# A two-layer hybrid encoder on one core: the softmax of the global branch in one pass, and where a few side operations stand

## The chip, the cores and the metric

The kernel runs on one core of a Trainium2 chip. The metric is device time in microseconds (us), the median of several executions; lower is better. The engines are TensorE (PE in the profile, with its weight loads as PEld), VectorE (DVE), ScalarE (ACT), GpSimd (POOL), and SyncE (SP), which here only issues DMAs. SBUF is the on-chip memory that all of them read; PSUM holds the sums that PE makes, in banks of 512 float32 columns.

## The reference

What is computed: two layers, each with one wide input projection, a grouped-query attention over all tokens, a neighbourhood attention in a window of 8 x 16 grid cells, and merge gates. There are 512 grid tokens and 16 meta tokens, the model is 1024 wide, and heads are 64 wide.

```python
def gqa_attention(q, k, v):
    scale = HEAD_DIM ** -0.5                       # 0.125
    def attend(qb):                                # a block of queries, against all 528 keys
        s = jnp.einsum('bqkgd,bskd->bkgqs', qb, k).astype(jnp.float32) * scale
        p = jax.nn.softmax(s, axis=-1).astype(v.dtype)
        return jnp.einsum('bkgqs,bskd->bqkgd', p, v)
...
def hybrid_layer(x, norm_g, w_in, q_norm_g, k_norm_g, rpb, w_o_attn, w_o_na, w_out, cos, sin):
    h = rms_norm(x, norm_g)
    proj = jnp.einsum('bld,de->ble', h, w_in)
    qa, ka, va, za, qb, kb, vb, zb, ga, gb = split_cols(proj)
    qa = apply_axial_rope(rms_norm(qa.reshape(b, l, ATTN_HEADS, HEAD_DIM), q_norm_g), cos, sin)
    ka = apply_axial_rope(rms_norm(ka.reshape(b, l, ATTN_KV_HEADS, HEAD_DIM), k_norm_g), cos, sin)
...
    oa = gqa_attention(qa, ka, va) * jax.nn.silu(za)
    ob = neighbourhood_attention(qb, kb, vb, rpb) * jax.nn.silu(zb)
    ya = jnp.einsum('ble,ed->bld', oa, w_o_attn)
    yb = jnp.einsum('ble,ed->bld', ob, w_o_na)
    mixed = jax.nn.sigmoid(ga) * ya + jax.nn.sigmoid(gb) * yb
    return x + jnp.einsum('bld,de->ble', mixed, w_out)
```

Everything is in float32.

## The kernel before

**The backbone.** All activations lie with features on the partitions and tokens along the columns. A projection (`product`, L277) makes 128 output features at a time: for each of eight blocks of input features three matmuls, L286 to L288, because weights and activations are split into a rounded high part and the rest (names ending in h and l, or hi and lo), and the product is high x high + high x low + low x high. The sum grows in a bank of the pool `ps_p` (two banks, named pp in the profile). A weight arrives by DMA (`raw`), ACT casts its high part (`whi`, L216) and GpSimd subtracts it for the low one (`wlo`, L217). A layer with 528 tokens runs each chunk as two halves of 264 columns, and where only the 512 grid tokens count, as one run of 512.

**The side work.** The attention branches are cut into short steps that are slipped between the projections. `product` calls `tick` after each half, and the two queues `side_na` (window heads) and `side_gqa` (global units) run what is due at that tick; tables (GQA_AT, NA_AT, NORM_AT at the top of the file) give the tick of each step within its unit, and `later(n, part)` puts a part n ticks on. A scheduler then sets the order on each engine from dependences and this order of code; `tc.high_priority()` lifts an instruction, and `tc.issue_after(x)` holds one behind x.

**The global branch.** A unit is one head and 256 queries: two softmaxes of 128 queries each (`softmax`, L697). PE writes the scores of 128 queries against 528 keys to S, the one tile of the pool `ps_s`, two banks wide (L499, L500, keys in KA0h/KA0l and so on). DVE takes the negated maximum of a row (L704) and multiplies it by the query's factor, a column of `r8` (L705; `r` in the profile); ACT reads S for the exponential with that factor and that maximum, writes P to SBUF and sums the row (L706); DVE inverts the sum (L708) and scales P (L709). PE transposes P (L116) into banks of the pool `ps_t` (two banks, named pt, ptm, and ta, tb, tc, vtb, vtd for other work that takes turns in them); ACT and DVE split a transposed bank into high and low part (`split`, L172 and L173, or `split_down`, L691 and L692), and PE sums with the values (L746). There are 64 softmaxes over both layers.

**The window branch.** A window head writes its scores to the same S, as Sb (called from L817), and its softmax is the one of L821 to L827: for each of four pieces, one DVE pass adds the bias, writes to SBUF and keeps the minimum, and ACT then does the exponential in SBUF. At the end of a head `sums` (L876) multiplies with the values, and `combine` (L672) adds the two halves of the result: ACT copies one half (L676), DVE adds (L677). After every second head `gated` (L679) multiplies by the gate and splits.

**The norms of queries and keys.** `head_roots` (L574) finds the inverse roots for all heads; `pair_factors` (L562) spreads those of the keys to 128 x 512 and 128 x 128 tiles (pfk, pfkm), and later those of the meta queries (pfq), by a copy on DVE (L566). PE transposes them (L601, L604) and DVE multiplies the keys by them (L602, L605). `stack_soon` (L481) then splits the keys of both pairs of heads, high part on ACT (L489), low part on DVE (L490), and two DMAs move what must lie on the other partitions. The projection of the window keys, `kb`, leaves its accumulator through DVE (L933 to L939), the queries `qb` through L943, and the gates through L663 (ACT then does the tanh, L664, and DVE a product, L669, that stands behind the newest maximum).

Of the kernel before, what the change touches and what calls it, by code (L numbers as in the profile page):

```python
# [18 lines left out]
P = 128  # L19
# [72 lines left out]
def trunk_kernel(ctx: ExitStack, tc: tile.TileContext, xT, w, gn, gf, bias, rope, out):  # L92
# [37 lines left out]
    nc.vector.memset(one, 1.0)  # L130
    nc.scalar.activation(one, one, AF.Exp)
    minus_half = cpool.tile([P, 1], F32, name="minus_half")
    nc.vector.memset(minus_half, -0.5)
# [137 lines left out]
    side_na, side_gqa = Side(NA_AT_TICK), Side(GQA_AT_TICK)  # L271

    def tick():
        side_na.tick()
        side_gqa.tick()

    def product(l, c, rhs, full, halves=(0, 1), name="pp", spans=None):  # L277
# [124 lines left out]
    for l in range(DEPTH):  # L402
# [77 lines left out]

        def stack_soon(tag, name, k, n):  # L481

            pairs = []
            for hh, r in enumerate((up, down)):
                kh, kl = slot(tag, f"{name}h{hh}", F32R), slot(tag, f"{name}l{hh}", F32R)
                for to in (up, down):
                    if hh and to is up:
                        continue
                    nc.scalar.copy(kh[to, :n], k[r, :n])  # L489
                    nc.vector.tensor_sub(kl[to, :n], k[r, :n], kh[to, :n].bitcast(F32))  # L490
# [71 lines left out]
        def pair_factors(t, c, n, name):  # L562

            f = slot("G", f"pf{name}{l}") if n > 1 else tiny.tile([P, P], F32, tag="pf", bufs=1, name=f"pf{name}{l}")
            f = f[:, :P * n].rearrange("p (n h d) -> p n h d", n=n, h=2)
            nc.vector.tensor_copy(f, st["r3"][:, t, c].rearrange("p t (n h) -> p (t n) h", h=2).unsqueeze(3)  # L566
                                  .to_broadcast([P, n, 2, HD]))
# [30 lines left out]
        def keys_scaled():  # L598
# [73 lines left out]
        def combine(tag, o, hh, av, c0, n):  # L672
# [3 lines left out]
            nc.scalar.copy(t[r, :n], av[q, :n])  # L676
            nc.vector.tensor_add(o[r, c0:c0 + n], av[r, :n], t[r, :n])  # L677

# [18 lines left out]
        def softmax(q, qs, kv, n, scale, name):  # L697
# [5 lines left out]
            with tc.high_priority():  # L703
                newest["max"] = nc.vector.tensor_reduce(st[:n, 0:1], S[:n, :, :HALF], axis=AX.XY, op=ALU.max, negate=True)  # L704
                nc.vector.tensor_scalar_mul(st[:n, 1:2], st[:n, 0:1], scale)  # L705
                nc.scalar.activation(p[:n].rearrange("p (i k) -> p i k", i=2), S[:n, :, :HALF], AF.Exp,  # L706
                                     bias=st[:n, 1:2], scale=scale, accum_out=st[:n, 2:3])
            nc.vector.reciprocal(st[:n, 3:4], st[:n, 2:3])  # L708
# [69 lines left out]
        def start_meta(kv):  # L778
            for j in (2 * kv, 2 * kv + 1):
                if j not in o_t:  # L780
                    o_t[j] = slot("T", f"oa{l}_{j}")
            return global_unit(kv, [(Q2m[kv], slice(0, 64), 0.125)], 64, f"m{l}_{kv}", lambda av: meta_done(kv, av))

# [14 lines left out]
        def windowed_head(hd):  # L798
# [77 lines left out]
            def sums():  # L876
# [7 lines left out]
                for i, (u, t, c0, a, b) in enumerate(seq):  # L884
                    nc.tensor.matmul(av[:, a:b], rows2(VB2[:, u, hh]), t[:, c0:c0 + b - a], start=i == 0,  # L885
                                     stop=i == len(seq) - 1, skip_group_check=True)
                combine("B", o, hh, av, 0, NREAL)
                if full:
                    av = bank(ps_t, f"avbm{nm}", "tp")
                    nc.tensor.matmul(av[:, :NMETA], rows2(VB2[:, 0, hh]), c["mt"], start=True, stop=True)  # L890
# [72 lines left out]
        for m in range(8 + LAG):  # L963
            if m < 8:
                gates[m] = merge_gate(GB, m)
            if m == LAG - 1:
                side_na.finish()
            if m >= LAG:
                mb.append(slot("B", f"mb{l}_{m - LAG}"))
# [143 lines left out]
```

## Time and profile before

| what | value |
|---|---|
| time, median of 3 | 878.3 us (878.14 to 878.75) |
| the profiled execution | 877.75 us |
| its span | 876.0 us |
| PE clock granted, mean | 0.997 of full speed |
| DVE busy, first layer, 25 to 300 us | 197.1 of 275.0 us |
| ACT busy in the same stretch | 159.3 of 275.0 us |
| DVE busy, second layer, 450 to 700 us | 182.8 of 250.0 us |
| ACT busy in the same stretch | 146.0 of 250.0 us |

A row of the timeline gives the start and the length of an instruction in us, its engine and line, its operation, the tile written and the tiles read, and their shapes; a bracket gives the idle time of that engine ahead of it and what ended it. A row of a group gives, behind its shapes, how many there are, their busy time in all and the mean in ns of one, and then the idle time of the engine ahead of them with what ended most of it. PE's matmuls overlap, so the distance of two starts says more than their lengths.

### The profile page before, as it was taken

The numbers are of one execution on the slowest core, as the hardware profiler recorded it, in microseconds if no ns is written. First come the engines' busy times: TensorE is split into PE (matmuls) and PEld (weight loads), VectorE is DVE, ScalarE is ACT, GpSimd is POOL, SyncE is SP. The second block draws the span as 40 slices with busy tenths as digits, with TensorE's granted clock in tenths as the row PEclk, the third lists the DMA queues.
The fourth block names the chain that finished last, engine by engine and source line by source line (L and its number), as shares of the span: only waits on it lengthen the run. The fifth ranks groups of instructions, "written<-read, shape, count | busy, mean of one in ns | idle before, by whom it ended". The sixth has DMA issues, their size and how long they took to land.

```text
span 876.0 us, 16169 instructions
## 1 busy us (share of the span) xinstructions
PE 858.6 (98%) x5984; PEld 791.1 (90%) x5984; DVE 556.8 (64%) x1264; ACT 462.3 (53%) x1027; POOL 364.0 (42%) x298
## 2 busy tenths in 40 slices
PE   9999999999999999999999999999999999999996
PEld 8999999999999999999998989888888888888785
DVE  6985678676774674436447757688867746544632
ACT  8644666565764554334345446566656645443422
POOL 5564343343233333454764643334332233334640
PEclk9999999999999999999999999999999999999998
DMA  8364444334222221324655654234432222222602
GB/s 278 109 161 123 112 120 118 89 110 122 73 71 74 73 74 61 109 86 143 168 129 128 158 160 129 79 109 133 124 109 73 76 81 73 85 84 97 205 24 97
DMA packets 67232, 96.90 MB, mean 111 GB/s; under 512 B 23376, under 2 KB 23888, under 8 KB 67152
## 3 DMA queue, kind: packets, MB, share of 16 engines
q1 hardware_dynamic: 66432, 94.79, 37.6%
q8 instruction: 47, 0.77, 0.4%
q10 hardware_dynamic: 720, 1.06, 0.3%
q14 instruction: 33, 0.27, 0.1%
HBM read 76.72 MB, written 4.19 MB: 92 GB/s over the span
## 4 chain that ended last, share of the span: by engine, by line
PE 83%; DVE 8%; ACT 5%; issue 2%; DMA 2%; POOL 0%; SPq 0%; POOLq 0%; ACTq 0%; DVEq 0%
PE pp L286 17%; PE pp L288 17%; PE pp L287 17%; PE y L288 3%; PE y L286 3%; PE y L287 3%; PE av L746 3%; PE pt L116 3%; PE avb L885 2%; PE S L500 2%; PE pf L1046 2%; PE pf L1048 2%; PE S L499 2%; PE pf L1047 1%; DVE Pb L827 1%
## 5 line engine op out<-in xcount | busy, mean ns | idle before, releaser
L217 POOL TENSOR_TENSOR wlo<-raw,whi 128x512 fp32r<-128x512 f32 x214 | 286.7, 1344 | 431.0 <-ACT whi L216 385.2
L286 PE MATMUL pp<-hh,whi 128*128 128x264 f32 (+1 forms) x1056 | 334.8, 317 | 1.8 <-DVE qb L943 1.0
L288 PE MATMUL pp<-hh,wlo 128*128 128x264 f32 (+1 forms) x1056 | 329.3, 312 | 0.0
L287 PE MATMUL pp<-hl,whi 128*128 128x264 f32 (+1 forms) x1056 | 328.2, 311 | 0.0
L216 ACT CAST whi<-raw 128x512 fp32r<-128x512 f32 x214 | 131.2, 620 | 157.6 <-PE pp L287 61.9
L286 PEld LDWEIGHTS pp<-hh,whi 128*128 128x128 f32 x1056 | 198.6, 188 | 12.0 <-DVE qb L943 1.2
L288 PEld LDWEIGHTS pp<-hh,wlo 128*128 128x128 f32 x1056 | 198.9, 188 | 10.8
L287 PEld LDWEIGHTS pp<-hl,whi 128*128 128x128 f32 x1056 | 199.3, 189 | 9.0
L706 ACT ACTIVATE P<-S,st,r 128x528 f32<-128x528 f32 x64 | 50.6, 790 | 52.7 <-DVE st L705 45.3
L953 DVE TENSOR_TENSOR mg<-pp,rbc 128x264 f32<-128x264 f32 (+1 forms) x48 | 24.8, 517 | 45.3 <-PE pp L288 44.5
L704 DVE TENSOR_REDUCE st<-S 128x1 f32<-128x528 f32 x64 | 45.0, 703 | 13.0 <-PE S L500 12.2
L173 DVE TENSOR_TENSOR ptl<-pt,pth 128x512 fp32r<-128x512 f32 x64 | 43.9, 687 | 13.1 <-ACT pth L172 12.6
L172 ACT CAST pth<-pt 128x512 fp32r<-128x512 f32 x64 | 37.3, 584 | 10.3 <-PE pt L116 9.3
L116 PE MATMUL pt<-ident,P 128*128 128x128 f32 x256 | 39.7, 274 | 2.0 <-DVE st L705 1.0
L708 DVE RECIPROCAL st<-st 128x1 f32<-128x1 f32 x64 | 10.5, 164 | 45.5 <-ACT P L706 45.1
L823 ACT ACTIVATE Pb<-Pb,stb 128x208 f32<-128x208 f32 (+1 forms) x64 | 31.0, 485 | 12.5 <-DVE stb L821 12.4
L287 PE MATMUL pp<-mxl,whi 128*128 128x264 f32 x128 | 36.5, 285 | 0.0
L286 PE MATMUL pp<-mxh,whi 128*128 128x264 f32 x128 | 36.5, 285 | 0.0
L288 PE MATMUL pp<-mxh,wlo 128*128 128x264 f32 x128 | 36.4, 284 | 0.0
L709 DVE TENSOR_SCALAR P<-P,st 128x528 f32<-128x528 f32 x64 | 34.7, 542 | 2.2
L954 ACT ACTIVATE mg<-mg 128x264 f32<-128x264 f32 (+1 forms) x48 | 23.7, 493 | 23.0 <-DVE mg L953 22.8
L746 PE MATMUL av<-pth,VA 128*128 128x256 f32 x128 | 35.1, 296 | 0.0
(611 smaller groups left out, 1765.7 us busy)
## 6 DMA issues: line engine op xcount, KB each, us to landing
raw<-in_w_dram SPq DMA_DIRECT2D x214, 256.0 KB, 2.7
bias<-in_bias_dram SPq DMA_DIRECT2D x16, 480.0 KB, 4.0
rawl<-in_w_dram SPq DMA_DIRECT2D x16, 256.0 KB, 3.1
x<-in_xT_dram SPq DMA_DIRECT2D x8, 264.0 KB, 4.6
xr<-in_xT_dram SPq DMA_DIRECT2D x8, 264.0 KB, 3.9
x1d<-xt SPq DMA_DIRECT2D x32, 64.0 KB, 2.8
xf<-x1d SPq DMA_DIRECT2D x8, 256.0 KB, 4.9
KB_0l<-kb SPq DMA_DIRECT2D x8, 140.0 KB, 2.6
```

The lines of the kernel that those rows point to most:

```text
L116: nc.tensor.transpose(ps, src, ident[:n, :n])
L172: split_at["hi"] = nc.scalar.copy(hi, src)
L173: split_at["any"] = nc.vector.tensor_sub(lo, src, hi.bitcast(F32))
L216: cast = nc.scalar.copy(hi, raw)
L217: sub = nc.gpsimd.tensor_sub(lo, raw, hi.bitcast(F32))
L286: nc.tensor.matmul(ps, wh, rh[:, a:b], start=i == 0, stop=False)
L287: nc.tensor.matmul(ps, wh, rl[:, a:b], start=False, stop=False)
L288: nc.tensor.matmul(ps, wl, rh[:, a:b], start=False, stop=i == n - 1)
L704: newest["max"] = nc.vector.tensor_reduce(st[:n, 0:1], S[:n, :, :HALF], axis=AX.XY, op=ALU.max, negate=True)
L706: nc.scalar.activation(p[:n].rearrange("p (i k) -> p i k", i=2), S[:n, :, :HALF], AF.Exp, bias=st[:n, 1:2], scale=scale, accum_out=st[:n, ...
L709: nc.vector.tensor_scalar_mul(p[:n], p[:n], st[:n, 3:4])
L746: nc.tensor.matmul(c["av"], rows2(c["t"][i][0]), c["t"][i][1], start=i == 0, stop=i == 8)
```

## The change

Six edits, all in the side work:

- `softmax`: the maximum, the scaling and the exponential are put together in another way. One DVE pass (L716 of the changed file) multiplies S by the query's factor, writes the product to P in SBUF and keeps the row's maximum; ACT negates the maximum (L719) and does the exponential from P to P (L720). For the units of meta queries, whose factor was the number 0.125, a tile `eighth` holds it.
- `pair_factors`: the spreading copies run on ACT.
- `stack_soon` handles one pair of heads at a time, and the second pair's call comes four ticks later.
- `combine`: the addition is held behind the newest maximum of a global softmax.
- `sums` of a window head: its collecting (combine, gated) is put off to the end of the tick, behind the global unit's steps of that tick.
- the transposed meta sums (`avbm`) are computed ahead of these additions.

```diff
+    eighth = cpool.tile([P, 1], F32, name="eighth")
+    nc.vector.memset(eighth, 0.125)
...
     def tick():
         side_na.tick()
         side_gqa.tick()
+        while ending:
+            ending.pop(0)()
...
-        def stack_soon(tag, name, k, n):
+        def stack_soon(tag, name, k, n, hh):
             pairs = []
-            for hh, r in enumerate((up, down)):
+            for hh, r in ((hh, (up, down)[hh]),):
...
-            nc.vector.tensor_copy(f, st["r3"][:, t, c].rearrange("p t (n h) -> p (t n) h", h=2).unsqueeze(3)
+            nc.scalar.copy(f, st["r3"][:, t, c].rearrange("p t (n h) -> p (t n) h", h=2).unsqueeze(3)
                                   .to_broadcast([P, n, 2, HD]))
...
-            KA2.extend(stack_soon("K", f"KA{l}", k, NTOK))
+            KA2.extend(stack_soon("K", f"KA{l}", k, NTOK, 0))
+            side_gqa.later(4, lambda: KA2.extend(stack_soon("K", f"KA{l}", k, NTOK, 1)))
...
             nc.scalar.copy(t[r, :n], av[q, :n])
-            nc.vector.tensor_add(o[r, c0:c0 + n], av[r, :n], t[r, :n])
+            with ExitStack() as held:
+                if "max" in newest:
+                    held.enter_context(tc.issue_after(newest["max"].ins))
+                nc.vector.tensor_add(o[r, c0:c0 + n], av[r, :n], t[r, :n])
...
             with tc.high_priority():
-                newest["max"] = nc.vector.tensor_reduce(st[:n, 0:1], S[:n, :, :HALF], axis=AX.XY, op=ALU.max, negate=True)
-                nc.vector.tensor_scalar_mul(st[:n, 1:2], st[:n, 0:1], scale)
-                nc.scalar.activation(p[:n].rearrange("p (i k) -> p i k", i=2), S[:n, :, :HALF], AF.Exp,
-                                     bias=st[:n, 1:2], scale=scale, accum_out=st[:n, 2:3])
+                newest["max"] = nc.vector.tensor_tensor_reduce(
+                    p[:n].rearrange("p (i k) -> p i k", i=2), S[:n, :, :HALF], scale[:n].unsqueeze(2).to_broadcast([n, 2, HALF]),
+                    1.0, -3e38, ALU.mult, ALU.max, st[:n, 0:1])
+                nc.scalar.mul(st[:n, 1:2], st[:n, 0:1], -1.0)
+                nc.scalar.activation(p[:n], p[:n], AF.Exp, bias=st[:n, 1:2], scale=1.0, accum_out=st[:n, 2:3])
...
-                combine("B", o, hh, av, 0, NREAL)
+                def collect(av=av):
+                    combine("B", o, hh, av, 0, NREAL)
+                    if full:
+                        combine("B", o, hh, c["avm"], NREAL, NMETA)
+                    if hh == 1:
+                        ob[j] = gated("M", o, zb[j], f"ob{l}_{j}")
                 if full:
...
-                    combine("B", o, hh, av[:, :NMETA], NREAL, NMETA)
-                if hh == 1:
-                    ob[j] = gated("M", o, zb[j], f"ob{l}_{j}")
+                    c["avm"] = bank(ps_t, f"avbm{nm}", "tp")[:, :NMETA]
+                    nc.tensor.matmul(c["avm"], rows2(VB2[:, 0, hh]), c["mt"], start=True, stop=True)
+                ending.append(collect)
```

How this moves instructions shows best at three places. The rows are those of the compiled order of one engine: line, operation, tile written, tiles read, shape; x3 stands for three in a row.

The first is DVE in layer 0 where the roots of the key norms are found (rh, tmh: Newton steps; kb: the window keys leaving their accumulator pp_14_264). Before:

```order
L566 COPY pfk_821<-rh_813 128x512
L566 COPY pfkm_823<-rh_813 128x128
L176 SCALAR_TENSOR_TENSOR tmh_816<-rh_813 128x40
L177 TENSOR_TENSOR tmh_816<-tmh_816,mh_812 128x40
L178 SCALAR_TENSOR_TENSOR rh_813<-tmh_816,rh_813 128x5x8
L176 SCALAR_TENSOR_TENSOR tmh_816<-rh_813 128x40
L177 TENSOR_TENSOR tmh_816<-tmh_816,mh_812 128x40
L936 TENSOR_TENSOR kb_0_766<-pp_14_264_840,rbc_345 128x56
L937 TENSOR_TENSOR kb_0_766<-pp_14_264_840,rbc_345 128x192
L939 TENSOR_TENSOR kb_0_766<-pp_14_264_840,rbc_345 128x16 x3
```

And in the changed program:

```order
L180 SCALAR_TENSOR_TENSOR rh_815<-tmh_818,rh_815 128x5x8
L178 SCALAR_TENSOR_TENSOR tmh_818<-rh_815 128x40
L179 TENSOR_TENSOR tmh_818<-tmh_818,mh_814 128x40
L180 SCALAR_TENSOR_TENSOR rh_815<-tmh_818,rh_815 128x5x8
L603 TENSOR_SCALAR r_0_833<-rh_815 128x32
L953 TENSOR_TENSOR kb_0_768<-pp_14_264_842,rbc_347 128x56
L954 TENSOR_TENSOR kb_0_768<-pp_14_264_842,rbc_347 128x192
L956 TENSOR_TENSOR kb_0_768<-pp_14_264_842,rbc_347 128x16 x3
L960 SCALAR_TENSOR_TENSOR qb_0_872<-pp_10_0_885,rbc_347 128x264
```

The two copies to pfk and pfkm have left DVE, and all Newton steps with the final factors r now stand ahead of kb.

The second is DVE in layer 0 at the end of window head 1, which a global softmax meets there (S_1_1_0 and its P_1_1_0; avb, avbm: the head's sums; vtb: transposed values; pt, ptl: a transposed P and its low part). Before:

```order
L677 TENSOR_TENSOR ob_0_1401<-avb_1_1965,cmb_1976 64x512
L704 TENSOR_REDUCE st_1_1_0_2012<-S_1_1_0_2007 128x1
L173 TENSOR_TENSOR VB_1_1990<-vtb_1_1992,VB_1_1990 128x6x64
L705 TENSOR_SCALAR st_1_1_0_2012<-st_1_1_0_2012,r_0_831 128x1
L677 TENSOR_TENSOR ob_0_1401<-avbm_1_1979,cmb_1982 64x16
L669 SCALAR_TENSOR_TENSOR za_1_1837<-za_1t,za_1_1837 128x528
L681 TENSOR_TENSOR ob_0_1401<-ob_0_1401,zb_0_1086 128x528
L173 TENSOR_TENSOR ptl_1_0_2_2004<-pt_1_0_2_1998,pth_1_0_2_2003 128x512
```

And in the changed program, where L716 is the fused pass (its second row reads the maximum out), L721 the reciprocal and L722 the scaling of P:

```order
L716 ISA P_1_1_0_2002,st_1_1_0_2001<-S_1_1_0_1996,r_0_833 128x528
L716 ISA st_1_1_0_2001 128x1
L175 TENSOR_TENSOR VB_1_1979<-vtb_1_1981,VB_1_1979 128x6x64
L688 TENSOR_TENSOR ob_0_1403<-avb_1_1967,cmb_2009 64x512
L721 RECIPROCAL st_1_1_0_2001<-st_1_1_0_2001 128x1
L688 TENSOR_TENSOR ob_0_1403<-avbm_1_1977,cmb_2013 64x16
L722 TENSOR_SCALAR P_1_1_0_2002<-P_1_1_0_2002,st_1_1_0_2001 128x528
L692 TENSOR_TENSOR ob_0_1403<-ob_0_1403,zb_0_1082 128x528
L175 TENSOR_TENSOR ptl_1_0_2_1993<-pt_1_0_2_1987,pth_1_0_2_1992 128x512
```

The additions of the head (L677, now L688) have moved behind the maximum, the split of vtb has moved up to it, and the reciprocal and scaling of the new P now stand ahead of the split ptl.

The third is ACT in layer 0 at window head 5 (ta: a transposed bank of that head, tah its high part; zb_3t: the tanh of a gate). Before:

```order
L691 CAST ga_118<-ptm_3_0_3192 32x256
L216 CAST whi_34_0_3272<-raw_34_0_3270 128x512
L664 ACTIVATE zb_3t<-zb_3_3137 128x264
L216 CAST whi_34_1_3278<-raw_34_1_3276 128x512
L172 CAST tah_5_3229<-ta_5_3224 128x512
L664 ACTIVATE zb_3t<-zb_3_3137 128x264
```

And in the changed program:

```order
L702 CAST ga_120<-ptm_3_0_3194 32x256
L218 CAST whi_34_0_3274<-raw_34_0_3272 128x512
L218 CAST whi_34_1_3280<-raw_34_1_3278 128x512
L174 CAST tah_5_3231<-ta_5_3226 128x512
L672 ACTIVATE zb_3t<-zb_3_3139 128x264 x2
```

The first half of the gate has moved from between the two weight casts to behind the cast of ta. In layer 1 the three low parts of the keys (KA1l, L490, now L497) keep their place on DVE ahead of the first qb. PE's order hardly changes, and GpSimd's not at all.

More of the change, by code (lines that the diff above doesn't have):

```diff
@@ L271, in trunk_kernel @@
     side_na, side_gqa = Side(NA_AT_TICK), Side(GQA_AT_TICK)
+    ending = []
     def tick():
@@ L781, in start_meta @@
                     o_t[j] = slot("T", f"oa{l}_{j}")
-            return global_unit(kv, [(Q2m[kv], slice(0, 64), 0.125)], 64, f"m{l}_{kv}", lambda av: meta_done(kv, av))
+            return global_unit(kv, [(Q2m[kv], slice(0, 64), eighth)], 64, f"m{l}_{kv}", lambda av: meta_done(kv, av))
         def start_unit(hd, i):
@@ L967, in trunk_kernel @@
                 side_na.finish()
+                while ending:
+                    ending.pop(0)()
             if m >= LAG:
```

2 lines of the change are left out of this document (removed).

## The prediction

> **What bounds the kernel now.** I read the busy times first, then the stretches at the start and the end, then the timeline of TensorE (PE) at each place where two matmuls start further apart than their neighbours do.
>
> ```profile
> span 876.0 us, 16169 instructions
> PE 858.6 (98%) x5984; PEld 791.1 (90%) x5984; DVE 556.8 (64%) x1264; ACT 462.3 (53%) x1027; POOL 364.0 (42%) x298
> ```
>
> ```profile
> 0.00:25.00 25.00, 22.81 (x164) 1.00 0.72 243
> 850.00:876.00 26.00, 19.05 (x83) 0.91 0.21 81
> ```
>
> The second fence is PE alone: length of the stretch, busy time, granted clock, DMA share, GB/s. PE is busy for 858.6 of 876.0 us, so it idles 17.4 us. Of these, 25.00 - 22.81 = 2.19 us lie in the first 25 us, before any softmax, and 26.00 - 19.05 = 6.95 us in the last 26 us, after the last one. The change touches neither stretch. What is left for it is 17.4 - 2.2 - 6.9 = 8.3 us of idle time of PE in the middle. No matmul is added or removed, and the granted clock is 1.00 where the work begins, so VectorE (DVE) and ScalarE (ACT) count only where PE waits for them. Saving busy time on DVE, which is busy 64% of the span, is worth nothing by itself.
>
> **How a wait is priced.** The trace shows the start of each matmul, and in a row with a bracket the idle time and what ended it.
>
> ```profile
> 86.47 0.28 PE L287 MATMUL pp<-hl,whi 128*128 128x264 f32 x1
> 86.59 0.28 PE L288 MATMUL pp<-hh,wlo 128*128 128x264 f32 x1
> 87.15 0.36 PE L499 MATMUL Sb<-KB_0h,QB_0a 128*128 128x208 f32 x1 [0.27 <-ACT P L706]
> ```
>
> ```profile
> 516.76 0.39 PE L287 MATMUL pp<-hl,whi 128*128 128x512 f32 x1
> 516.99 0.40 PE L288 MATMUL pp<-hh,wlo 128*128 128x512 f32 x1
> 517.67 0.36 PE L499 MATMUL Sb<-KB_0h,QB_0a 128*128 128x208 f32 x1 [0.28 <-ACT P L706]
> ```
>
> ```profile
> 604.95 0.40 PE L288 MATMUL pp<-hh,wlo 128*128 128x512 f32 x1
> 606.00 0.36 PE L499 MATMUL Sb<-KB_2h,QB_2a 128*128 128x208 f32 x1 [0.66 <-ACT P L706]
> ```
>
> Undisturbed, a matmul follows one of 264 columns after 0.12 us (86.47 to 86.59) and one of 512 after 0.23 us (516.76 to 516.99). The first window score at 87.15 comes 0.56 us after the matmul before it, so 0.44 us is lost there; at 517.67 it is 0.68 - 0.23 = 0.45 us, at 606.00 1.05 - 0.23 = 0.82 us. All three end when the exponential of L706 has read the score bank: that bank, S, exists once, and a head's window scores need it next.
>
> **Part A: the softmax.** Before, DVE takes the maximum from S (L704), scales it (L705), and ACT reads S once more for the exponential (L706). After, one DVE pass reads S, writes the scaled scores to SBUF and keeps their maximum, so S is free when that pass ends; ACT negates the maximum and does the exponential in place.
>
> ```profile
> L704 DVE TENSOR_REDUCE st<-S 128x1 f32<-128x528 f32 x64 | 45.0, 703 | 13.0 <-PE S L500 12.2
> L705 DVE TENSOR_SCALAR st<-st,r 128x1 f32<-128x1 f32 x64 | 13.2, 206 | 0.9
> L706 ACT ACTIVATE P<-S,st,r 128x528 f32<-128x528 f32 x64 | 50.6, 790 | 52.7 <-DVE st L705 45.3 <-DVE ob L677 4.4 <-PE y L288 1.4
> L706 ACT ACTIVATION_READ_ACCUMULATOR P<-S,st,r 128x1 f32 x64 | 12.2, 190 | 0.0
> L821 DVE CUSTOM_DVE_ANT_0 Pb<-Sb,bias 128x272 f32<-128x272 f32 x32 | 12.8, 436 | 0.0
> L821 DVE CUSTOM_DVE_ANT_0 Pb<-Sb,bias 128x208 f32<-128x208 f32 x32 | 11.9, 372 | 6.0 <-PE Sb L500 3.9 <-PE sm L500 2.0
> L821 DVE DVE_READ_ACCUMULATOR2_ANT stb<- 128x1 f32 x64 | 5.3, 83 | 0.0
> L823 ACT ACTIVATE Pb<-Pb,stb 128x272 f32<-128x272 f32 x32 | 16.3, 509 | 0.0
> L131 ACT ACTIVATE one<-one 128x1 f32<-128x1 f32 x1 | 0.2, 203 | 0.0
> ```
>
> The window heads already run such a fused pass (L821): 372 ns for 208 columns and 436 for 272 make 1.0 ns a column, so 528 columns cost 372 + 320 = 692 ns, and 83 for reading the maximum out. The exponential from SBUF is L823: 509 ns for 272 columns. Its slope is bounded from the longer row: if all the 790 - 509 = 281 ns were columns, 1.1 ns a column; the trace's slope for 208 to 272 columns is lower, so I take 700 ns, between 509 and 790. A one-column pass on ACT cost 203 ns (L131). The chain from scores to finished exponential is then 692 + 83 + 203 + 700 + 190 = 1868 ns, against 703 + 206 + 790 + 190 = 1889 ns: no change. DVE gains 703 + 206 - 775 = 134 ns a softmax, ACT loses 203 + 700 - 790 = 113 ns. S is released after 775 ns instead of 703 + 206 + 790 = 1699 ns, at least 0.9 us sooner. That is more than each of the three waits, so they vanish: 0.44 + 0.45 + 0.82 = 1.71 us. What is late next is what DVE splits for PE (below, the rows of L692), which this edit does not hasten; I keep 0.7 of it: **1.2 us**, bounds 0 and 1.7. Against it stands the finished P, which the transposes of L116 wait for:
>
> ```profile
> L116 PE MATMUL pt<-ident,P 128*128 128x128 f32 x256 | 39.7, 274 | 2.0 <-DVE st L705 1.0 <-DVE P L709 0.9
> ```
>
> PE already idles 0.9 us for P in all. A second hand-over inside ACT and casts that stand between its one-column product and the exponential can add to that; a doubled wait would be -0.9, none 0. I take **-0.4 us**.
>
> **Part B: pair factors on ACT.** In layer 0 the factor copies stand on DVE between the norm's Newton steps and the evacuation of kb, which frees the accumulator that PE needs at 58.23.
>
> ```profile
> L566 DVE COPY pfk<-rh x2: 429/968/1508, 53.7 to 493.6; 128x512 f32<-128x512 f32 x2
> L566 DVE COPY pfkm<-rh x2: 221/766/1310, 55.1 to 493.9; 128x128 f32<-128x128 f32 x2
> ```
>
> ```profile
> 57.41 0.27 PE L604 MATMUL rkm<-ident,pfkm 128*128 128x128 f32 x1
> 58.23 0.36 PE L286 MATMUL pp<-hh,whi 128*128 128x264 f32 x1 [0.55 <-DVE rh L178]
> ```
>
> ```profile
> 61.27 0.37 PE L499 MATMUL S<-KA0h,Q_0a 128*128 128x264 f32 x1
> 62.00 0.39 PE L500 MATMUL S<-KA0l,Q_0a 128*128 128x264 f32 x1 [0.37 <-DVE KA0l L490]
> ```
>
> The two copies of layer 0 take 1.51 and 1.31 us there, 2.8 us of DVE right ahead of the accumulator's evacuation. Without them it is ready long before PE asks: 58.23 - 57.41 - 0.12 = 0.70 us goes. The stack of keys (KA0l) is at the end of the same queue, so 62.00 - 61.27 - 0.12 = 0.61 us goes as well. The copies cost ACT as much as its other 512-column copies, and ACT is not what PE waits for there. Together **1.3 us**; bounds 0, if the copies on ACT come late for the transposes of L601, and 1.3.
>
> [...]
>
> **Part C: the sums of a window head held behind the newest maximum.** Before, at the end of head 1 of layer 0 the addition L677 stands ahead of the maximum, and that ahead of the split of VB, whose bank the transposes pt take next.
>
> ```profile
> 133.11 0.56 DVE L173 TENSOR_TENSOR VB<-vtb,VB 128x384 fp32r<-128x384 f32 x1
> ```
>
> ```profile
> 132.52 0.28 PE L288 MATMUL pp<-hh,wlo 128*128 128x264 f32 x1
> 133.81 0.63 PE L116 MATMUL pt<-ident,P 128*128 128x128 f32 x4 [1.02 <-DVE st L705]
> ```
>
> ```profile
> 136.13 0.40 PE L116 MATMUL ptm<-ident,P 128*32 128x128 f32 x2
> ```
>
> The bracket names L705, but the split that ends at 133.67 is what frees the bank; 133.81 - 132.52 - 0.12 = 1.17 us is lost. After, the fused pass runs in DVE's idle time before L677 and the split follows at once, so about 1.0 us is won. But the next split (ptl) now stands behind the reciprocal and the scaling of the new P, which wait for the exponential. I put its end at 135.6 (an estimate: exponential's end 133.3, then 0.16, 0.54, 0.70 and 0.69 us of DVE work with gaps), and ptm at 136.13 needs its bank. Only 0.4 to 0.5 us is kept: **0.4 us**, bounds 0 and 1.1.
>
> **Part D: the second key pair's stack, four ticks later.**
>
> ```profile
> L490 DVE TENSOR_TENSOR KA0l<-k,KA0h x3: 701/706/707, 60.5 to 62.1; 64x528 fp32r<-64x528 f32 x3
> ```
>
> ```profile
> 499.69 4.40 DVE L490 TENSOR_TENSOR KA1l<-k,KA1h 64x528 fp32r<-64x528 f32 x3 [0.79 <-ACT KA1h L489]
> ```
>
> ```profile
> 503.62 0.28 PE L288 MATMUL pp<-hh,wlo 128*128 128x264 f32 x1
> 504.87 0.39 PE L286 MATMUL pp<-hh,whi 128*128 128x264 f32 x1 [0.96 <-DVE qb L943]
> ```
>
> In layer 1 three subtractions take 4.40 us where those of layer 0 take 3 x 0.71 = 2.12, and qb queues behind them: 504.87 - 503.62 - 0.12 = 1.13 us. The issue order of the changed program still has all three ahead of qb in layer 1; only in layer 0 does qb overtake one. So what can help is that DVE arrives earlier (two copies fewer) and meets GpSimd's subtractions elsewhere. Bounds 0 and 1.13; I take half, **0.6 us**. The two stacking DMAs that go later with it feed keys that are first read several units later, so they hide behind those.
>
> **Part E: ACT's order at head 5.**
>
> ```profile
> 213.74 0.28 PE L288 MATMUL pp<-hh,wlo 128*128 128x264 f32 x1
> 214.54 0.50 PE L116 MATMUL tc<-ident,Pb 128*32 128x128 f32 x3 [0.53 <-DVE tal L173]
> ```
>
> PE waits for the split of ta (tal). Its cast is late on ACT, since a gate (zb_3t), whose tile a DMA still reads, stands two places before it; 214.54 - 213.74 - 0.12 = 0.68 us is lost. In the new order both halves of the gate stand behind the cast of ta: **0.6 us**, bounds 0 and 0.7.
>
> **Part F: the window heads' third transposes.**
>
> ```profile
> 584.72 0.29 PE L641 MATMUL vtd<-ident,vb 128*32 128x128 f32 x1 [0.79 <-DVE na L692]
> ```
>
> ```profile
> 623.18 0.28 PE L641 MATMUL vtd<-ident,vb 128*32 128x128 f32 x1 [0.36 <-DVE na L692]
> ```
>
> At the first place the scaling of P moves ahead of a projection's evacuation and the 0.79 us goes; at the second, five small evacuations move ahead of it and I put the same 0.8 us on it. Net **0**, bounds -0.8 and +0.8.
>
> **The sum.** 1.2 - 0.4 + 1.3 + 0.4 + 0.6 + 0.6 + 0 = 3.7 us. The profiled execution took 877.75 us (its span and 1.75 us around it), so 874.05 by its clock; the median shown, 878.3, is 0.55 above it, so 874.6 us. The one-column tile (`eighth`) costs one set-up instruction in PE's idle first microseconds: nothing.
>
> **The rivals.**
> 1. *The waits only move.* PE reaches the next wait on DVE sooner and waits there; parts A, C, D and E come to nothing and only B stays, since behind it lies no wait for several microseconds: 878.3 - 1.3 = 877.0 us. For it: every row of L692 and L116 above is ended by DVE. Against it: between these waits lie tens of microseconds without one, so a shift of 0.5 us is not simply met again. Chance 0.18.
> 2. *The stack is not later.* The edit named for the second key pair does not act in layer 1 and D falls away: 878.3 - 3.1 = 875.2 us. For it: the order of DVE there. Against it: the copies leave DVE in any case. Chance 0.15.
> 3. *Slower: the fused pass is slow.* At 528 columns, over two banks and with a broadcast column as second operand, it is not the operation of L821, which reads a full tile. If it took 2 ns a column, 1.1 us and more, each of 64 softmaxes would hold DVE about 0.5 us longer, 32 us on top of 556.8, and P would come 0.4 us later. With two transposes in each of some 32 units that stand close behind P, a 0.2 us wait in each makes 6.4 us: 874.6 + 6.4 = 881.0 us. It decides from about 1.1 us a pass; below 0.9 it is hidden. Against it: 1.0 ns a column in both rows of L821. Chance 0.07.
> 4. *All of it comes*, with no wait taking over: at most the 8.3 us of idle time, 870.0; by the upper ends 1.7 + 1.3 + 1.1 + 1.1 + 0.7 + 0.8 = 6.7 us, 871.6. Chance 0.08.
>
> A rule that bears on part D: the Trainium skill, page "SBUF — State Buffer", section "Who interferes with whom", says that a DVE instruction with two SBUF inputs and a GpSimd one that reads SBUF exclude each other, and that the order of issue decides who waits. By it D is all or nothing, 1.1 or 0 us, so 874.1 or 875.2. The 4.40 against 2.12 us agrees that something held DVE, not which.
>
> **Chances.** The forecast, 872.5 to 876.3, has 0.52; with rivals 2 and 4 and less its own tail, faster has 0.70. A measurement of this kernel tells 0.2% (1.8 us) from no change, so rival 1 is "same", with the forecast's tail 0.23; slower 0.07. The range reaches from just below the upper ends of the terms to just above no change: 870.8 to 878.4.
>
> **What would show it.** Right for A: no wait on Sb ended by a softmax, and a fused pass of 0.69 us; for B: no gap at 58 us; for C: a pt at 133 us with 0.2 us of gap and a new one before ptm; for D: qb at 504 us sooner; for E: tc at 214 us without a gap. PE's idle time would fall from 17.4 to about 13.7 us. Wrong would be: a fused pass above 0.9 us, new gaps at transposes that wait for P, or the same idle time at other places.

## The result and the profile after

The changed kernel takes 870.79 us (median of 4 runs, 870.57 to 871.04) against 878.52 us (878.14 to 879.82, now four runs): a ratio of 0.9909, 95% interval 0.9892 to 0.9927, or 7.7 us less. The forecast was 874.6 us and its range began at 870.8. The direction was right; the gain was twice the forecast, and as large as I allowed for rival 4, to which I gave 0.08.

The page's first rows, and PE's stretches at the two ends (length, busy time, clock, DMA share, GB/s):

```profile
span 868.8 us, 16164 instructions
PE 855.9 (99%) x5984; PEld 791.5 (91%) x5984; DVE 537.5 (62%) x1260; ACT 475.6 (55%) x1098; POOL 362.9 (42%) x298
```

```profile
0.00:25.00 25.00, 22.62 (x160) 1.00 0.74 243
842.80:868.80 26.00, 19.02 (x83) 0.95 0.22 81
```

PE's idle time fell from 17.4 to 868.8 - 855.9 = 12.9 us, by 4.5, and the two ends kept theirs (2.4 and 7.0 us). The span fell by 7.2. The other 2.7 us left PE's *busy* time, because a wait is longer than the idle time that the profile books for it. The record of the matmul ahead lasts 0.28 us, though the next can start 0.12 us after it: ahead of the window score at 87.15 the bracket says 0.27 us where the starts say 0.44. And a matmul that starts after a wait is recorded as longer (0.36 to 0.40 us in the rows of waits), and the next follows it later:

```profile
87.35 0.28 PE L500 MATMUL Sb<-KB_0l,QB_0a 128*128 128x208 f32 x1
87.46 0.31 PE L499 MATMUL Sb<-KB_0h,QB_0a 128*128 128x272 f32 x1
```

That is 0.20 us after 87.15, and then 0.11 us. So part of each wait counts as work, idle time was no full measure of what waits cost, and my bound of 8.3 us for "all of it" was not a bound.

To see where the 7.2 us come from, I paired the 4416 matmuls of projections and merges in both traces, in order, and noted by how much the changed kernel's lead grows from one to the next. From 20 us on it grows by 7.6 us; before that it lost 0.4 us, which lies ahead of every changed part. The steps of 0.15 us and more, by the parts of the prediction:

| part | forecast, us | measured | where |
|---|---|---|---|
| A, window scores no longer wait for S | 1.2 | 2.5 | 89, 518, 607, 678 us: 0.55, 0.56, 0.94, 0.43 |
| A, transposes of P | -0.4 | -0.1 | 72 us -0.92; 317 and 326 us +0.62, +0.18 |
| F, the window heads' third transposes | 0 | 1.6 | 585 and 589 us 0.91, 0.21; 623 us 0.46 net |
| B, factors on ACT | 1.3 | 1.4 | 58 and 62 us: 0.79, 0.64 |
| C, sums behind the maximum | 0.4 | 0.2 | 132 to 136 us 0.35; 226 to 229 us -0.12 |
| D, second stack | 0.6 | 0.7 | 505 us |
| E, ACT's order at head 5 | 0.6 | 0.65 | 215 us |
| not named | 0 | 0.7 | 536 us 0.22; 684 us 0.23; 694 and 695 us -0.71, +0.49; 147 and 182 us -0.16, +0.18; the rest small steps |

Times there are those of the kernel before. The pair at 694 and 695 us is a change of order alone: the next scores are computed ahead of three merge matmuls. Of the 0.62 us at 317, some 0.28 is not the softmax's: the four kernels below that keep the old softmax gain that much there too, so it belongs to the one trace of the kernel before.

Three rows of PE in the changed kernel answer to rows shown before: tc at head 5, pt at head 1, and the qb place in layer 1.

```profile
212.82 0.61 PE L116 MATMUL tc<-ident,Pb 128*32 128x128 f32 x4
```

```profile
132.16 0.63 PE L116 MATMUL pt<-ident,P 128*128 128x128 f32 x4 [0.43 <-DVE VB L175]
```

```profile
501.05 0.28 PE L295 MATMUL pp<-hh,wlo 128*128 128x264 f32 x1
501.63 0.39 PE L293 MATMUL pp<-hh,whi 128*128 128x264 f32 x1 [0.30 <-DVE qb L960]
```

The first has no bracket any more; the other two still wait, for 0.43 and 0.30 us where it was 1.02 and 0.96.

The groups of the new softmax (busy time, mean ns | idle of the engine ahead, what ended it):

```profile
L716 DVE CUSTOM_DVE_ANT_1 P<-S,r 128x528 f32<-128x528 f32 x64 | 45.1, 705 | 14.4 <-PE S L507 13.4
L716 DVE DVE_READ_ACCUMULATOR2_ANT st<- 128x1 f32 x64 | 5.3, 83 | 0.0
L719 ACT ACTIVATE st<-st 128x1 f32<-128x1 f32 x64 | 12.9, 202 | 29.6 <-DVE st L716 28.8
L720 ACT ACTIVATE P<-P,st 128x528 f32<-128x528 f32 x64 | 47.1, 737 | 1.8
```

The durations are what the sum used: 705 for 692, 202 for 203, 737 for 700. Yet paired instance by instance, from the start of the maximum to the end of the scaled P takes 2.72 us on average over the 66 softmaxes (64 of 128 queries, two of the 64 meta queries), where it took 3.26. The difference sits between the maximum's end and the exponential's start: 0.40 us instead of 0.85. DVE and ACT at the softmax ahead of the third window head of layer 1 show it, before:

```profile
603.57 0.71 DVE L704 TENSOR_REDUCE st<-S 128x1 f32<-128x528 f32 x1
604.31 0.42 DVE L692 TENSOR_TENSOR tbh<-tb,tbh 64x256 fp32r<-64x256 f32 x1
604.76 0.21 DVE L705 TENSOR_SCALAR st<-st,r 128x1 f32<-128x1 f32 x1
```

```profile
605.07 0.79 ACT L706 ACTIVATE P<-S,st,r 128x528 f32<-128x528 f32 x1 [1.65 <-DVE st L705]
```

and after:

```profile
598.68 0.71 DVE L716 CUSTOM_DVE_ANT_1 P<-S,r 128x528 f32<-128x528 f32 x1
599.32 0.08 DVE L716 DVE_READ_ACCUMULATOR2_ANT st<- 128x1 f32 x1
599.43 0.42 DVE L703 TENSOR_TENSOR tbh<-tb,tbh 64x256 fp32r<-64x256 f32 x1
```

```profile
599.43 0.20 ACT L719 ACTIVATE st<-st 128x1 f32<-128x1 f32 x1 [1.23 <-DVE st L716]
599.67 0.74 ACT L720 ACTIVATE P<-P,st 128x528 f32<-128x528 f32 x1
```

```profile
600.05 0.26 PE L506 MATMUL Sb<-KB_2h,QB_2a 128*128 128x208 f32 x1
```

Before, another head's split (tbh, 0.42 us) stands in DVE's queue between the maximum and its scaling; the exponential starts 605.07 - 603.57 = 1.50 us after the maximum did. After, the same split stands behind both, and the exponential starts 599.67 - 598.68 = 0.99 us after. S is free at 599.4, 0.7 us after the pass began, and the window score at 600.05 waits for nothing.

So the open question was: why is the softmax worth so much more than the terms I gave it, and by which of two mechanisms? **S**: its bank is free sooner. **Q**: the hand-over no longer needs a second place in DVE's queue.

### The profile page after: what moved, and what is told of

It reads as the page before. It is cut to its first block, busy times and chain, and to the rows that moved or that the text cites. A ratio compares the mean times of both kernels' runs of the same rounds, so it can differ in the third digit from the quotient of the medians.

```text
span 868.8 us, 16164 instructions
## 1 busy us (share of the span) xinstructions
PE 855.9 (99%) x5984; PEld 791.5 (91%) x5984; DVE 537.5 (62%) x1260; ACT 475.6 (55%) x1098; POOL 362.9 (42%) x298
## 4 chain that ended last, share of the span: by engine, by line
PE 87%; DVE 4%; ACT 3%; DMA 2%; issue 2%; SPq 1%; POOL 0%; POOLq 0%; DVEq 0%; ACTq 0%
PE pp L293 18%; PE pp L295 18%; PE pp L294 18%; PE av L759 4%; PE y L293 4%; PE y L295 4%; PE y L294 3%; PE pt L116 3%; PE avb L898 2%; PE S L506 2%; PE S L507 2%; PE pf L1065 2%; PE pf L1067 2%; PE pf L1066 1%; DMA x<-in_xT_dram 1%
## 5 line engine op out<-in xcount | busy, mean ns | idle before, releaser
L716 DVE CUSTOM_DVE_ANT_1 P<-S,r 128x528 f32<-128x528 f32 x64 | 45.1, 705 | 14.4 <-PE S L507 13.4
L720 ACT ACTIVATE P<-P,st 128x528 f32<-128x528 f32 x64 | 47.1, 737 | 1.8
L722 DVE TENSOR_SCALAR P<-P,st 128x528 f32<-128x528 f32 x64 | 32.0, 501 | 2.1
L759 PE MATMUL av<-ptl,VA 128*128 128x256 f32 x128 | 33.0, 280 | 0.0
```

Of the source, the lines that this page charges most:

```text
L716: newest["max"] = nc.vector.tensor_tensor_reduce(p[:n].rearrange("p (i k) -> p i k", i=2), S[:n, :, :HALF], scale[:n].unsqueeze(2).to_broa ...
L720: nc.scalar.activation(p[:n], p[:n], AF.Exp, bias=st[:n, 1:2], scale=1.0, accum_out=st[:n, 2:3])
L722: nc.vector.tensor_scalar_mul(p[:n], p[:n], st[:n, 3:4])
L759: nc.tensor.matmul(c["av"], rows2(c["t"][i][0]), c["t"][i][1], start=i == 0, stop=i == 8)
```

## The experiments

Each ratio is against the kernel before on the same chip. A difference between two changed kernels is one of medians that can come from different chips, on which the kernel before took 878.19 to 878.70 us, so it is good to about half a us; where one matters, the paired traces' figure (the lead from 20 us on) stands beside it.

### One part at a time

Only the new softmax (with `eighth`), from the kernel before:

```diff
-                newest["max"] = nc.vector.tensor_reduce(...)
-                nc.vector.tensor_scalar_mul(st[:n, 1:2], st[:n, 0:1], scale)
-                nc.scalar.activation(p[:n]..., S[:n, :, :HALF], AF.Exp, bias=st[:n, 1:2], scale=scale, ...)
+                newest["max"] = nc.vector.tensor_tensor_reduce(p[:n]..., S[:n, :, :HALF], scale..., 1.0, -3e38, ALU.mult, ALU.max, st[:n, 0:1])
+                nc.scalar.mul(st[:n, 1:2], st[:n, 0:1], -1.0)
+                nc.scalar.activation(p[:n], p[:n], AF.Exp, bias=st[:n, 1:2], scale=1.0, ...)
```

> The kernel before with the new softmax alone (and its tile eighth). Theory Q (the gain is the removed wait in DVE's queue between maximum and exponential, and S released sooner by that as well): from the maximum's start to P's end takes about 2.7 us on average instead of 3.26; the waits at the window scores (2.5 us in the changed kernel's drift), at the transposes of P (0.8) and at the third transposes of layer 1 (1.5) go with this part alone: 4 to 5 us, 873.5 to 874.5. Theory F (the forecast's sizes: S sooner is worth 1.2 us, the chain is no shorter): 877 to 878.

Measured: 873.40 us (873.22 to 874.14), ratio 0.9941 (0.9929 to 0.9954): 5.3 us by this part alone (4.6 in the paired traces). The forecast's sizes are out; the softmax is where most of the gain is. The steps at 89, 317, 326, 518, 585, 589, 607 and 678 us are in its trace as in the table above; at 215 us it loses 0.61.

Only the pair factors on ACT:

```diff
-            nc.vector.tensor_copy(f, st["r3"]...
+            nc.scalar.copy(f, st["r3"]...
```

> The kernel before with the pair factors copied on ACT, nothing else. Both theories: the gaps at 58 and 62 us go (1.3 to 1.4 us). If what is won there is met again at the first transposes of P near 72 us, as in the changed kernel, where 0.9 us is lost at that place, only about 0.5 us is left: 877.8 to 878.1. If it stays: 877.0 to 877.3. In layer 1, DVE without the two copies lets qb at 504 us come up to 0.6 us sooner if that gap hung on them.

Measured: 878.07 us (876.95 to 879.85), ratio 0.9997 (0.9988 to 1.0006): no difference that can be told. Its trace has the steps of 0.79 and 0.63 us at 58 and 62 us in full, and then loses 1.78 at the first transposes of P. PE and ACT there:

```profile
73.50 0.52 PE L116 MATMUL pt<-ident,P 128*128 128x128 f32 x3 [1.84 <-DVE P L709]
```

```profile
71.04 0.62 ACT L216 CAST whi<-raw 128x512 fp32r<-128x512 f32 x1 [3.79 <-DMA raw<-in_w_dram]
71.57 0.79 ACT L706 ACTIVATE P<-S,st,r 128x528 f32<-128x528 f32 x1
```

The exponential stands in ACT's queue behind a weight cast, and that waits for a DMA. PE came sooner, P did not. Some of the 1.78 can be this execution's: the kernels with the stack alone and the sums alone, whose edits don't touch this place, lose 0.29 and 0.42 there; all eight traces that have the factors on ACT and the casts as they were lose 0.6 to 1.8. One step stays: 0.66 us at 505 us, the one that I had put down to the second stack.

Only the second key pair's stack later:

```diff
-            KA2.extend(stack_soon("K", f"KA{l}", k, NTOK))
+            KA2.extend(stack_soon("K", f"KA{l}", k, NTOK, 0))
+            side_gqa.later(4, lambda: KA2.extend(stack_soon("K", f"KA{l}", k, NTOK, 1)))
```

> The kernel before with the second key pair's stack four ticks later, nothing else. Forecast's term D, 0.6 us, if the gap before qb at 504 us hangs on this edit; none there if the order of DVE in layer 1 is what counts. In layer 0 at most the 0.6 us at 62 us. 877.7 to 878.5.

Measured: 878.90 us (878.28 to 879.31), ratio 1.0001 (0.9992 to 1.0010). No step at 505 us: this edit does nothing there, as rival 2 had it, and the wait went with the factors.

Only the window head's sums, held and collected at the end of the tick, with the transposed meta sums ahead of them:

```diff
+                    held.enter_context(tc.issue_after(newest["max"].ins))
                 nc.vector.tensor_add(o[r, c0:c0 + n], av[r, :n], t[r, :n])
...
-                combine("B", o, hh, av, 0, NREAL)
...
+                ending.append(collect)
```

> The kernel before with the window head's sums held behind the newest maximum and collected at the end of the tick, nothing else. Both theories: the gap at 214 us goes (0.65), since the cast of ta stands ahead of both halves of the gate; at 133 us 0.3 to 1.0 us is won. 877.0 to 877.7. Theory Q adds: without the fused pass the maximum's scaling still waits in DVE's queue, so the waits for Sb (517, 606 us) stay.

Measured: 877.43 us (876.96 to 878.14), ratio 0.9986 (0.9977 to 0.9995): 0.4 to 2.0 us. The step of 0.65 us at 215 us is there, and 0.6 us net from 132 to 134 us; the waits for S stay.

### One part taken out

The changed kernel with the old softmax:

> The changed kernel with the old softmax (factors, stack and collecting as in the change). If the parts add up, it takes the time of before less what e2, e3 and e4 gave (0.6, -0.2 and 1.3): 876.8 to 877.2. If the collecting is worth more with the fused softmax than without, it is slower than that, 877.3 to 878.5.

Measured: 876.71 us (876.09 to 877.67), ratio 0.9982 (0.9973 to 0.9991). The other parts together are worth what they gave singly, and the softmax is worth 876.71 - 870.79 = 5.9 us within the changed kernel (6.5 in the paired traces).

The changed kernel with the additions at their old place:

> The changed kernel with the additions of a head at their old place (neither held behind the maximum nor put off to the end of the tick). If the parts add up, 870.8 + 1.3 = 872.1. In the softmax alone the place at 214 us lost 0.6 us and that at 132 us 1.5 us, which the changed kernel does not: if the additions undo those losses, 872.3 to 873.2; the gap at 214 us is then about 1.3 us wide.

Measured: 872.03 us (871.66 to 872.92), ratio 0.9931 (0.9918 to 0.9943): 1.2 us more than the changed kernel (1.1 in the paired traces), about what the sums gave alone.

The changed kernel with both stacks at the old tick:

> The changed kernel with both pairs' stacks at the old tick. Alone the edit gave nothing (878.9 against 878.7), so 870.6 to 871.2; more than 1 us slower if it matters only together with the others (the first score at 61 us, which then waits for the low part of the keys).

Measured: 871.22 us (870.85 to 871.42), ratio 0.9912 (0.9899 to 0.9926): not to be told from the changed kernel.

### S or Q

The exponential reads S again, so that S is held until it ends; the negation stays on ACT:

```diff
-                nc.scalar.activation(p[:n], p[:n], AF.Exp, bias=st[:n, 1:2], scale=1.0, accum_out=st[:n, 2:3])
+                nc.scalar.activation(p[:n].rearrange("p (i k) -> p i k", i=2), S[:n, :, :HALF], AF.Exp, bias=st[:n, 1:2], scale=scale[:n], accum_out=st[:n, 2:3])
```

> The changed kernel, but its exponential reads S again (with the factor as pointer) instead of P: the scores' bank is held until the exponential ends, while the negation stays on ACT. It parts two mechanisms. If the gain of the softmax came from S being free sooner (mechanism S), the waits of the window scores come back in part and 1.5 to 2.5 us are lost: 872.3 to 873.5. If it came from the missing wait in DVE's queue between maximum and exponential (mechanism Q), S is held only about 2.1 us instead of 2.67, the 0.3 to 0.5 us gaps at 517 and 606 us mostly stay away, and little is lost: 870.8 to 871.8.

The negation on DVE, S free early:

```diff
-                nc.scalar.mul(st[:n, 1:2], st[:n, 0:1], -1.0)
+                nc.vector.tensor_scalar_mul(st[:n, 1:2], st[:n, 0:1], -1.0)
```

> The changed kernel, but the one-column negation runs on DVE instead of ACT: S is still freed by the fused pass, but the exponential again waits for a second place in DVE's queue. Mechanism S: nothing is lost, 870.5 to 871.3. Mechanism Q: from the maximum's end to the exponential's start takes about 0.8 us instead of 0.4 on average, transposes of P and the third transposes of layer 1 wait again, 1.5 to 3 us are lost: 872.3 to 873.8.

Measured: 872.41 us (872.10 to 873.07), ratio 0.9934 (0.9922 to 0.9947), for the first, and 871.12 us (870.86 to 871.55), ratio 0.9919 (0.9906 to 0.9933), for the second. Undoing S costs 1.6 us; undoing Q costs 0.3, far from the 1.5 to 3 that I expected of it, though the chain did grow: 3.18 us on average instead of 2.72. Both times lie in the ranges that I had written down for S. But together the two are 1.9 of 5.9 us (2.3 of 6.5 in the paired traces), so S is not the whole either, and both theories as I had put them fell. The third was that either is nearly enough by itself, tested by both at once (the two edits above together):

> The changed kernel with both at once: the exponential reads S (S held until it ends) and the negation runs on DVE. Each alone cost little (1.6 and 0.3 us), together 1.9, while the whole new softmax is worth 5.9 us in the changed kernel (876.71 without it). If the two are independent causes: 872.7 and the rest of the 5.9 us is something third (one DVE operation less, another order). If they are alternatives, each enough by itself to keep S from being held long (theory R): 875.5 to 877, with the waits of Sb at 89, 518 and 678 us back.

Measured: 876.47 us (876.09 to 876.62), ratio 0.9973 (0.9962 to 0.9984). That is the time without the new softmax (876.71): though the fused pass is still there, nothing of the gain is left. The waits of the weight loads for the window scores show how, in the view of waits (in all, times, longest): of the kernel before,

```profile
PEld Sb L499 <- ACT P L706: 3.5, 8, 1.1
```

of the kernel with S held,

```profile
PEld Sb L506 <- ACT P L720: 1.2, 3, 0.9
```

and of the kernel with both undone:

```profile
PEld Sb L506 <- ACT P L720: 4.4, 8, 1.0
```

With the negation on DVE alone, and in the changed kernel, there is no such row. A window score needs S at a certain time. It is met when S is let go before the exponential, whenever that comes, and nearly always when the exponential comes soon. Only when it is late *and* holds S does PE wait. The third transposes depend on the chain instead. The steps of 0.15 us and more at the two kinds of place, and the lead over the kernel before, in us:

| kernel | window scores (89, 518, 607, 678 us) | third transposes (585, 589, 623, 627 us) | lead |
|---|---|---|---|
| changed | 2.5 | 1.6 | 7.6 |
| S undone | 1.8 | 1.5 | 6.0 |
| Q undone | 2.5 | 0.1 | 6.9 |
| both undone | 0 | -0.4 | 1.8 |
| old softmax | -0.2 | 0.2 | 1.1 |

So the small cost of undoing Q is a net figure: 1.5 us go at the third transposes, where I had looked for them, and 0.6 come back at 136 and 229 us, where the weight loads for the transposes ptm no longer wait (0.7 us in all in the changed kernel's view of waits). Undoing both loses 5.8 us, of which the two columns hold 4.5; I did not follow the rest.

At 585 us (in the time of before) it is the scaling of P that is late. In the kernel before it stands behind a projection's evacuation, and runs long:

```profile
582.32 1.30 DVE L709 TENSOR_SCALAR P<-P,st 128x528 f32<-128x528 f32 x1
```

```profile
582.03 1.29 POOL L217 TENSOR_TENSOR wlo<-raw,whi 128x512 fp32r<-128x512 f32 x1 [3.35 <-ACT whi L216]
```

In the changed kernel it stands ahead, and the transposes wait for nothing:

```profile
576.86 0.49 DVE L722 TENSOR_SCALAR P<-P,st 128x528 f32<-128x528 f32 x1
```

```profile
579.70 0.28 PE L649 MATMUL vtd<-ident,vb 128*32 128x128 f32 x1
```

With the negation on DVE it is behind the evacuation again (576.92), runs 1.30 us, and the wait is back. In both traces with the 1.30 us GpSimd does a subtraction of 1.29 us at that time, and in the one with 0.49 none; that the one slows the other no run here tests. In the views of waits, of the changed kernel and of the one with the negation on DVE:

```profile
PEld vtd L649 <- DVE na L703: 2.1, 4, 0.7
```

```profile
PEld vtd L649 <- DVE na L703: 3.7, 5, 1.2
```

### The wait that part B met

In the changed kernel the transposes of P at 72 us wait 0.95 us, and ACT shows the same order as above:

```profile
72.34 0.55 PE L116 MATMUL pt<-ident,P 128*128 128x128 f32 x3 [0.95 <-DVE P L722]
```

```profile
69.97 0.62 ACT L218 CAST whi<-raw 128x512 fp32r<-128x512 f32 x1 [3.02 <-DMA raw<-in_w_dram]
70.49 0.20 ACT L719 ACTIVATE st<-st 128x1 f32<-128x1 f32 x1
70.72 0.74 ACT L720 ACTIVATE P<-P,st 128x528 f32<-128x528 f32 x1
```

The fused pass and the reading of its maximum end at 69.13, but negation and exponential stand behind the cast. Two kernels hold casts behind the newest exponential, the first all of them; the second adds `and (l_, c_) == (0, ZA)` to the condition, which leaves the two casts of one weight:

```diff
-            cast = nc.scalar.copy(hi, raw)
+            with ExitStack() as held:
+                if "exp" in split_at:
+                    held.enter_context(tc.issue_after(split_at["exp"].ins))
+                cast = nc.scalar.copy(hi, raw)
...
+                split_at["exp"] = nc.scalar.activation(p[:n], p[:n], AF.Exp, ...)
```

> The changed kernel with every weight cast on ACT held behind the newest exponential. At 72 us the transposes of P wait 1.1 us because negation and exponential stand behind a weight cast that itself waits; here they stand ahead of it. If that reading is right, the gap at 72 us goes, 0.9 us. Held everywhere, casts may come late for PE elsewhere: 869.8 to 872.5.

> As e12, but only for the one weight (the first gate chunk of layer 0) whose casts stand in front of that exponential. 0.9 us faster than the changed kernel, 869.7 to 870.2, if nothing behind it takes the wait over; 870.6 to 871.0 if the next one does.

Measured: 878.67 us (877.15 to 879.81), ratio 0.9997 (0.9989 to 1.0006), for all casts, and 869.52 us (869.09 to 870.26), ratio 0.9894 (0.9881 to 0.9908), for the one. ACT and PE of the second:

```profile
69.00 0.20 ACT L722 ACTIVATE st<-st 128x1 f32<-128x1 f32 x1 [3.04 <-DVE st L719]
69.23 0.74 ACT L723 ACTIVATE P<-P,st 128x528 f32<-128x528 f32 x1
69.87 0.19 ACT L723 ACTIVATION_READ_ACCUMULATOR P<-P,st 128x1 f32 x1
69.97 1.12 ACT L221 CAST whi<-raw 128x512 fp32r<-128x512 f32 x2
```

```profile
70.96 0.60 PE L116 MATMUL pt<-ident,P 128*128 128x128 f32 x4
```

The exponential fits into the time in which the cast waited for its DMA; the gap is gone and nothing takes it over. This is the fastest median of the study, 1.3 us below the changed kernel; the intervals of the two ratios overlap, but in the paired traces the lead from 20 us on grows by 8.8 us instead of 7.6, and 1.2 of that (a step of +0.25 instead of -0.92) lies at this place. Holding all casts wins the same at 72 us and loses some 9 us elsewhere (878.67 against 869.52 us), far outside the 869.8 to 872.5 that I expected. One such place, at 222 us, where the exponential itself started 4.2 us after its maximum, behind a gate that waited 2.27 us for a DMA:

```profile
222.25 0.55 PE L116 MATMUL pt<-ident,P 128*128 128x128 f32 x3 [1.87 <-DVE P L725]
```

More of the loss stands at transposes (pt, ptm) that wait for the split ptl: 2.5 and 2.4 us of PE in the view of waits, where the changed kernel has no such row of PE. Why those splits come late I did not follow.

## Why the prediction was wrong, point by point

- **What bounds the kernel** was right: PE, and the others only where PE waits. Its bound, "8.3 us of idle time of PE in the middle", was too small a measure of the waits, since part of them is booked as busy; the forecast of 13.7 us of idle time (12.9 measured) hid that.
- **Part A is the step that failed.** "The chain from scores to finished exponential is then ... no change" added up five durations that were each right to some 40 ns, and left out that L705 was an entry of its own in DVE's queue, with other work between it and the maximum. From the maximum's start to the exponential's end, ahead of the reading of its sum, the instances took 2.34 us on average before, not 1.70, and 1.84 after. Up to the scaled P the chain became 0.54 us shorter, so the -0.4 us for transposes of P was near only by a cancellation (+0.80 at two places, -0.92 at one, which came with the factors: the softmax alone has -0.18 there). The 1.2 us for S was mis-sized as well: I took three waits of four, priced each 0.11 us too low (they came to 2.05 us, not 1.71, since PE is slower behind a wait as well), and kept 0.7 of them for "What is late next"; the rows that I pointed at for that stand at other places. The four were 2.5 us, and none came back. That shortening and the early release are alternatives for the window scores is shown by the pair of kernels and their combination (+1.6, +0.3, and together +5.7 us), and by the rows of the table there.
- **Part F** failed with it: "0" was 0.8 us won at one place and 0.8 us lost at the other. The loss was an opinion on an order of rows. At the second place kb's evacuations ran while DVE had nothing else to do. 0.5 us was won there and 1.1 at the first. About 0.2 of the 0.5 is not the softmax's but the sums': the steps at 623 us are those of the kernel with the sums alone, and the one with the softmax alone lacks them.
- **Part B** was right in size at its place (1.4 for 1.3), and rival 1's mechanism was right for it: in the factors alone 1.78 us was lost again 10 us later, 0.92 in the changed kernel. I had said that behind it "lies no wait for several microseconds"; a wait ten microseconds on was enough.
- **Parts C and E** were right within 0.2 us, C with its give-back at ptm.
- **Part D** was right in size (0.7 for 0.6) and wrong in cause: the factors' leaving DVE did it, the later stack did nothing measurable. The three subtractions of layer 1, in the view of their line (shortest, median, longest in ns), still run long in the changed kernel, but one of them does not:

```profile
L497 DVE TENSOR_TENSOR KA1l<-k,KA1h x3: 706/1254/1818, 496.9 to 499.0; 64x528 fp32r<-64x528 f32 x3
```

  So "all or nothing", which I had drawn from the Trainium skill (page "SBUF — State Buffer", section "Who interferes with whom"), holds at most for each instruction by itself, not for the three together.
- **The negation on ACT** is the slower one by its duration: 202 ns, and 146 on DVE. The kernel was no slower for it (870.79 against 871.12 us), and with S held it was 4.1 us faster (872.41 against 876.47 us). The place counted, not the 56 ns.
- **The rivals.** Slower by a slow fused pass was out: 705 ns. Rival 1 happened at one place only. Rival 2's condition came true, the later stack did nothing, but its price did not, since the factors gave those 0.66 us. The time is within rival 4's, yet by waits that the sum didn't have, and with one taking over at 72 us.
- **The measurement.** The profiled execution of before was 0.55 us under the median shown, which I added to the forecast. Its first 20 us were among the short ones (below), so the gain by medians, 7.7, is the 7.6 that the traces show from there on.

## What to carry to other kernels

An operation costs its duration and its place: two halves of a chain on one engine, with another engine's work ready to slip between them, are priced by the time from the first one's start to the last one's end in the trace, instance by instance, and not by the sum of their means. Take a discount for what is late next only with a row that shows the next wait and how close it is; where none is near, the whole wait is won, and where one is, look what its input stands behind, since moving that one instruction may be worth more than the edit. And if a gain survives each of two undoings, undo both before calling either unimportant, and look at the places too: a small net cost can be a loss at one and a gain at another.

## What was not expected of the hardware

- The first 20 us differ between executions of nearly the same program: the same matmul of the third chunk started at 19.15 us before, at 19.55 in the changed kernel, and between 19.1 and 20.5 in the others. Two traces are better compared from there on.
- A fused multiply and maximum over two banks, with a column spread along the free axis as second operand, took 705 ns for 528 columns, the same as the plain maximum (703).
- A one-column product on DVE took 206 ns with its factor in memory (L705) and 146 with a constant (the negation).
